# Attention scores from rounded fp32 in two passes, in a tuned trunk layer

## The chip, the cores and the metric

The kernel runs on one core of a Trainium2 chip. The metric is the device time of one execution in microseconds (us); the times of a kernel are given as the median of its runs.

## The reference

One layer of a trunk over 512 latent tokens with 256 context tokens, model width 1024, all in fp32. A normalised input is projected once into three branches (a gated width-3 convolution, a two-way diagonal state-space layer, and neighbourhood attention), which are gated, merged and projected; a squared-ReLU MLP with 4096 hidden columns follows. The change touches the scores of the attention alone:

```
s_loc = jnp.einsum('bqhd,bwkhd->bhqwk', q_r, k_r).astype(jnp.float32) * scale + bias
s_loc = jnp.where(key_in[:, None, :], s_loc, NEG_INF)
s_ctx = jnp.einsum('bqhd,bchd->bhqc', q_r, kch).astype(jnp.float32) * scale
s = jnp.concatenate([s_loc..., s_ctx], axis=-1)
p = jax.nn.softmax(s, axis=-1)
```

There are 8 heads of 64 channels. Each query sees a window of latent keys and all 256 context keys.

## The kernel before

Nearly all matrix products are made from *rounded fp32* (dtype fp32r, which PE takes in one pass, at some loss of low bits). To keep the precision, `split` (line 90) writes a value as a rounded high part and a rounded low part (the value less its high part), and `mm3` (line 98) adds three products into one accumulator: high x high, high x low, low x high (lines 99, 100, 101). Weights come from memory as a stream of 128 x 1024 blocks (`raw`); `wsplit` makes their high part on ACT (line 171) and their low part on DVE (line 174), two units ahead of use.

The work is a list of *units* (`unit_list`), one per 128 output columns. `slot` takes them in turn: it prepares weights for the unit after next, pumps the side streams, evacuates the unit before (`flush`, which calls `ev_unit`), and issues the unit's matmuls in two halves (`mm_unit`). The attention's units come as q, k, v for j = 0 to 3; each j holds two heads, one on partitions 0 to 63, the other on 64 to 127. A unit's result stands in one of three accumulators of 512 columns (`pm`, tag "m"); k and v take two each, one for the latent and one for the context tokens.

The attention itself is a side stream (`ATT.gen`, rate 3), in 16 steps n, four blocks i of 128 queries for each j. A step makes scores (line 788: two key ranges, a window of 192 or 256 keys and the 256 context keys, for each of the two heads), adds the bias with a running maximum (DVE, line 792), takes the exponential (ACT, line 801), transposes (line 814) and multiplies with v (line 829). The transposes of v are at line 754. The scores of before are plain fp32 matmuls over 64 rows of the array: q and k stand as fp32 tiles of 128 partitions, and each head uses its half of them. `ev_unit` writes these tiles: q by one ACT instruction (line 964), k by one on ACT (line 968) and one on DVE (line 969).

The order of each engine's instructions is fixed when the program is built: a planner takes, at each point of its own estimate of the run, the first instruction of the program order whose operands and buffers are ready. So side streams and units interleave on PE, and a changed instruction can change the order of others.

A "64 x 128" matmul here is one that uses 64 rows (input partitions) and 128 columns (output partitions) of PE's array; "128 x 64" one that uses all rows and half of the columns. The trace shows a plain fp32 score matmul as two instructions with two weight loads.

Of the kernel before, what the change touches and what calls it, by code (L numbers as in the profile page):

```python
# [9 lines left out]
F32 = mybir.dt.float32  # L10
F32R = mybir.dt.float32r
I32 = mybir.dt.int32
AF = mybir.ActivationFunctionType
# [3 lines left out]
MUL, ADD, SUB = ALU.mult, ALU.add, ALU.subtract  # L17

D = 1024
T = 512  # L20
# [55 lines left out]
def trunk(tc, xT, ctxT, cond, condT, vecs, wst, s5p, s5bc, dmat, biasA, outT):  # L76
# [3 lines left out]
    V, S, P, PE = nc.vector, nc.scalar, nc.gpsimd, nc.tensor  # L80

    def f(ap):
        return ap.bitcast(F32)
# [6 lines left out]
    def split(hi, lo, src, scale=None, eng=None):  # L90
        if scale is None:
            S.copy(hi, src)  # L92
            (eng or V).tensor_tensor(lo, src, f(hi), op=SUB)  # L93
        else:
            S.activation(hi, src, AF.Copy, scale=scale)
            V.scalar_tensor_tensor(lo, src, scale, f(hi), op0=MUL, op1=SUB)
# [7 lines left out]
    with es:  # L104
# [8 lines left out]
        def pm(name, n=T):  # L113
            return pp.tile([128, 512], F32, tag="m", bufs=3, name=name)[:, :n]

        def pa(name):
            return pp.tile([128, 1024], F32, tag="a", bufs=2, name=name)

        def pss(name):
            return pp.tile([128, 512], F32, tag="s", bufs=1, name=name)  # L120
# [38 lines left out]
        late = {}  # L159
# [39 lines left out]
        cs = cp.tile([128, 8, 2], F32, name="cs")  # L199
# [198 lines left out]
        for c in range(4):  # L398
# [7 lines left out]
            for t in range(4):  # L406
                o = 2 * t + c // 2
# [334 lines left out]
        qkv = {}  # L742

        class ATT:
# [19 lines left out]
            def gen(self):  # L764
                units = [(j, i) for j in range(4) for i in range(4)]
                bia = {}

                bt = [late["paf"].tile([128, 2, 512], F32, name=f"bt{e}") for e in range(2)]
                for t in bt:
                    P.memset(t[:, :, 256:512], 0.0)  # L770

                def load_bias(n):
                    if n < 16:
                        j, i = units[n]
                        t = bt[n % 2]
                        o = 2 * sum(NK[:i])
                        nc.sync.dma_start(t[:, :, 256 - NK[i]:256], biasA[j][:, o:o + 2 * NK[i]].rearrange("p (h m) -> p h m", h=2))
                        bia[n] = t

                def scores(n):  # L780
                    j, i = units[n]
                    nk, k0 = NK[i], K0[i]
                    q, k = qkv["q", j], qkv["k", j]
                    ps = pa(f"sps{n}").rearrange("p (h m) -> p h m", h=2)
                    for c0, c1, o in ((k0, k0 + nk, 256 - nk), (512, 768, 256)):
                        for h in range(2):
                            r = slice(64 * h, 64 * h + 64)
                            PE.matmul(ps[:, h, o:o + c1 - c0], q[r, 128 * i:128 * i + 128], k[r, c0:c1], start=True, stop=True)  # L788
                    mx = tp.tile([128, 4], F32, tag="mx", bufs=2, name=f"mx{n}")
                    for h in range(2):  # L790
                        sl = ps[:, h, 256 - nk:512]
                        V.tensor_tensor_reduce(out=sl, in0=sl, in1=bia[n][:, h, 256 - nk:512], scale=1.0, scalar=-3.0e38,
                                               op0=ADD, op1=ALU.max, accum_out=mx[:, h:h + 1])
                    V.tensor_scalar(mx[:, 0:2], mx[:, 0:2], -1.0, None, op0=MUL)
                    return ps, mx

                def soft(n, ps, mx):
                    nk = NK[units[n][1]]
                    pr = self.p.tile([128, 2, 512], F32, tag="pr", bufs=2, name=f"pr{n}")
                    for h in range(2):  # L800
                        self.ex[n] = S.activation(pr[:, h, 256 - nk:512], ps[:, h, 256 - nk:512], AF.Exp, bias=mx[:, h:h + 1], accum_out=mx[:, 2 + h:3 + h])
                    V.reciprocal(mx[:, 2:4], mx[:, 2:4])
                    for h in range(2):
                        V.tensor_scalar(pr[:, h, 256 - nk:512], pr[:, h, 256 - nk:512], mx[:, 2 + h:3 + h], None, op0=MUL)
                    return pr

                def transp(n, pr):
                    i = units[n][1]
                    nk = NK[i]
                    ps = pa(f"ptps{n}").rearrange("p (h t m) -> p h t m", h=2, t=4)  # L810
                    offs = (256 - nk, 128 if i != 3 else 192, 256, 384)
                    for h in range(2):
                        for t, o in enumerate(offs):
                            PE.transpose(ps[:, h, t], pr[:, h, o:o + 128], ident)  # L814
                    pt = self.p.tile([128, 2, 4, 128], F32, tag="pt", bufs=2, name=f"pt{n}")
                    S.copy(pt[:, 0], ps[:, 0])
                    V.tensor_copy(pt[:, 1], ps[:, 1])
                    return pt

                def values(n, pt):  # L820
                    j, i = units[n]
                    v = qkv["v", j]
                    ops = pss(f"ops{n}")[:, :128]
                    tiles = {0: ((0, 64), (1, 128)), 1: ((1, 128), (2, 128)), 2: ((2, 128), (3, 128)), 3: ((3, 128), (4, 64))}[i]
                    tiles += ((5, 128), (6, 128))
                    for t, (vt, rows) in enumerate(tiles):
                        for h in range(2):
                            r = slice(64 * h, 64 * h + 64)
                            PE.matmul(ops[r], v[:rows, vt, r], pt[:rows, h, t], start=t == 0, stop=t == 3, skip_group_check=True)  # L829
                    if i == 0:  # L830
                        self.of[j] = self.p.tile([128, 512], F32, tag="of", bufs=1, name=f"of{j}")
                    of = self.of[j]
                    S.copy(of[:, 128 * i:128 * i + 128], ops)
                    if i == 3:
                        split(*oo(j), of)

                load_bias(0)
                prev = None
                vps = None
                for n in range(17):  # L840
                    if n < 16:
                        while any((a, units[n][0]) not in qkv for a in ("vt", "q", "k")):
                            yield
                        load_bias(n + 1)

                    if vps is not None:
                        self.vsp(vps)
                        vps = None
                    if n < 16:
                        sc = scores(n)  # L850
                    if prev is not None:
                        pt = transp(n - 1, prev)
                    yield

                    if n < 16 and units[n][1] == 0:
                        vps = units[n][0]
                        self.vtr(vps)
                    if n < 16:
                        nxt = soft(n, *sc)
                    if prev is not None:  # L860
                        values(n - 1, pt)
                    prev = nxt if n < 16 else None
                    yield
# [4 lines left out]
        res = {}  # L868
# [11 lines left out]
        def oo(k):  # L880
            return gpair(6, 7, k) if k < 2 else hx(4 + k)
# [49 lines left out]
        def ev_unit(u):  # L931
            kind, j = u
            ps = res.get(u)
# [26 lines left out]
                    m = 2 * j + i  # L960
                    V.scalar_tensor_tensor(fg(m), gt["ga", m], 1.0, res[u, i], op0=ADD, op1=MUL)
            elif kind == "q":
                q = late["pa"].tile([128, T], F32, tag="q", bufs=2, name=f"q{j}")
                S.activation(q, ps, AF.Copy, scale=0.125)
                qkv[u] = q
            elif kind == "k":
                k = late["pa"].tile([128, 768], F32, tag="k", bufs=2, name=f"k{j}")
                S.copy(k[:, 0:512], ps)
                V.tensor_copy(k[:, 512:768], res[u, "c"])
                qkv[u] = k  # L970
            elif kind == "v":
                vt = tp.tile([128, 768], F32, tag="vt", bufs=1, name=f"vt{j}")
# [31 lines left out]
            elif kind == "m2":  # L1004
                c, m, h = j
# [91 lines left out]
        def flush():  # L1097
            if pending[0] is not None:
                u = pending[0]
                pending[0] = None  # L1100
                ev_unit(u)
# [20 lines left out]
        i = 0  # L1122
# [107 lines left out]
        for h, cs in enumerate(HALF):  # L1230
            for m in range(3, 8):
                ps = pm(f"wo{m}_{h}", 256)
# [5 lines left out]
        for h, cs in enumerate(HALF):  # L1238
# [11 lines left out]
            for j in range(4):  # L1250
# [3 lines left out]
                ps = pm(f"m1_{j}_{h}", 256) if j < 3 else pss(f"m1_{j}_{h}")[:, :256]  # L1254
# [9 lines left out]
        for h, cs in enumerate(HALF):  # L1264
            for m in (6, 7):
                ps = pm(f"m2e{m}_{h}", 256)
# [11 lines left out]
            else:  # L1278
# [8 lines left out]
                for t in range(2):  # L1287
                    ob = lp.tile([128, 1024], F32, tag="wl", bufs=3, name=f"ob{t}")
                    for e in range(2):
                        src, dst = ots[t][:, 512 * e:512 * e + 512], ob[:, 512 * e:512 * e + 512]  # L1290
# [145 lines left out]
```

## Time and profile before

| | us |
|---|---|
| median of 3 runs | 1051.85 (1051.36 to 1053.2) |
| the profiled execution | 1054.51 |
| its span in the trace | 1052.7 |

| engine | busy us | share of the span |
|---|---|---|
| PE (matmul) | 1004.4 | 95% |
| PEld (weight load) | 810.2 | 77% |
| DVE | 558.9 | 53% |
| ACT | 366.7 | 35% |
| POOL | 200.7 | 19% |

The span runs from the first to the last instruction of the program. PE's matmuls overlap in the trace (each one's duration includes its way through the array), so the time that a matmul takes from PE is read from start to start. The attention's matmuls lie between 434 and 610 us.

### The profile page before, as it was taken

What the parts mean: (1) busy time and instruction counts of PE and PEld (TensorE: products, weight loads), DVE (VectorE), ACT (ScalarE), POOL (GpSimd) and SP (SyncE); (2) the same over time, 40 slices, a digit from 0 to 9 for tenths busy, and PEclk for the clock granted to TensorE, in tenths of its full rate; (3) what the DMA queues carried; (4) which work ended last, traced back from release to release, by engine and by line L of the source; (5) the groups of instructions that cost most, each with busy time, mean ns of one, the idle gap of its engine ahead of it and who ended that gap; (6) DMA issues with size and microseconds to landing.
All of it is one profiled execution on the core that took longest, in us unless ns stands there. A gap on an engine that the chain in (4) does not pass through costs nothing.

```text
span 1052.7 us, 13485 instructions
## 1 busy us (share of the span) xinstructions
PE 1004.4 (95%) x5358; PEld 810.2 (77%) x5358; DVE 558.9 (53%) x927; ACT 366.7 (35%) x586; POOL 200.7 (19%) x159
## 2 busy tenths in 40 slices
PE   5889996989899999999999999999999999999997
PEld 2457885978788787777777778998888888888887
DVE  6733789348963144465467876566442234443322
ACT  5123422332222233354346444345331113333311
POOL 0555144546661013220020200000000000000000
PEclk9999999899799999999999999999999999999999
DMA  8355334785446456443254465223323223232202
GB/s 308 130 195 175 123 135 177 172 285 179 142 156 205 143 204 227 179 145 105 71 184 139 149 233 188 81 81 126 115 81 110 90 80 120 80 103 98 80 1 80
DMA packets 64543, 149.38 MB, mean 142 GB/s; under 512 B 28864, under 2 KB 41152, under 8 KB 52064
## 3 DMA queue, kind: packets, MB, share of 16 engines
q1 hardware_dynamic: 47792, 138.99, 38.4%
q10 hardware_dynamic: 16688, 9.53, 3.2%
q8 instruction: 42, 0.69, 0.3%
q14 instruction: 21, 0.17, 0.1%
HBM read 130.16 MB, written 18.32 MB: 141 GB/s over the span
## 4 chain that ended last, share of the span: by engine, by line
PE 74%; DMA 8%; DVE 8%; POOL 5%; issue 3%; ACT 2%; SPq 1%; ACTq 0%; DVEq 0%; POOLq 0%
PE m L99 10%; PE m L100 10%; PE m L101 10%; PE mod L511 3%; PE ops L829 2%; DMA raw<-in_wst_dram 2%; DMA C_d<-c 2%; PE sps L788 2%; PE ptps L814 2%; PE wo L100 1%; PE wo L99 1%; PE wo L101 1%; DVE v L681 1%; DVE wl L174 1%; DMA ks<-KT_d 1%
## 5 line engine op out<-in xcount | busy, mean ns | idle before, releaser
L174 DVE TENSOR_TENSOR wl<-raw,wh 128x1024 fp32r<-128x1024 f32 x144 | 187.6, 1303 | 226.1 <-ACT wh L171 224.4
L171 ACT CAST wh<-raw 128x1024 fp32r<-128x1024 f32 x144 | 150.9, 1049 | 314.6 <-PE m L100 151.1
L99 PE MATMUL m<-rg,wh 128*128 128x512 f32 (+1 forms) x480 | 184.2, 385 | 0.0
L101 PE MATMUL m<-rg,wl 128*128 128x512 f32 (+1 forms) x480 | 183.9, 384 | 0.0
L101 PEld LDWEIGHTS m<-rg,wl 128*128 128x128 f32 x480 | 90.1, 188 | 19.1
L99 PEld LDWEIGHTS m<-rg,wh 128*128 128x128 f32 x480 | 89.9, 188 | 18.7
L100 PE MATMUL m<-rg,wh 128*128 128x512 f32 (+1 forms) x256 | 96.4, 378 | 0.0
L100 PE MATMUL m<-actl,wh 128*128 128x512 f32 x224 | 87.8, 392 | 0.0
L1065 POOL TENSOR_TENSOR junk<-raw,silx 128x1024 f32<-128x1024 f32 x16 | 45.4, 2838 | 215.5 <-DMA raw<-in_wst_dram 214.2
L100 PEld LDWEIGHTS m<-rg,wh 128*128 128x128 f32 x256 | 48.0, 188 | 8.6
L511 PE MATMUL mod<-raw,cs 128*2 128x256 f32 x128 | 35.0, 432 | 17.9 <-DMA raw<-in_wst_dram 10.9
L100 PEld LDWEIGHTS m<-actl,wh 128*128 128x128 f32 x224 | 42.0, 187 | 9.8
L511 PEld LDWEIGHTS mod<-raw,cs 128*2 128x2 f32 x128 | 11.2, 92 | 38.1 <-issue 15.9
L1069 DVE SCALAR_TENSOR_TENSOR jk<-raw,silx 128x1024 bf16<-128x1024 f32 x16 | 21.8, 1362 | 32.5 <-DMA raw<-in_wst_dram 32.5
L1020 DVE SCALAR_TENSOR_TENSOR fg<-m,mod,fg 128x512 f32<-128x512 f32 x14 | 10.5, 751 | 52.8 <-PE m L101 52.8
L681 DVE TENSOR_TENSOR_SCAN v<-r,v 128x96 f32<-128x96 f32 x64 | 29.5, 523 | 15.1 <-POOL v L673 15.1
L92 ACT CAST rg<-relu 128x512 fp32r<-128x512 f32 (+1 forms) x36 | 20.3, 575 | 38.6 <-DVE relu L1013 38.6
L93 DVE TENSOR_TENSOR actl<-relu,rg 128x512 fp32r<-128x512 f32 (+1 forms) x36 | 22.3, 630 | 18.5 <-ACT rg L92 18.5
L100 PE MATMUL wo<-rg,wh 128*128 128x256 f32 (+1 forms) x104 | 31.8, 309 | 0.0
L99 PE MATMUL wo<-rg,wh 128*128 128x256 f32 (+1 forms) x104 | 31.8, 307 | 0.0
L101 PE MATMUL wo<-rg,wl 128*128 128x256 f32 (+1 forms) x104 | 31.5, 306 | 0.0
L829 PE MATMUL ops<-pt,v 128*64 128x128 f32 (+1 forms) x256 | 31.3, 287 | 0.0
(426 smaller groups left out, 2309.0 us busy)
## 6 DMA issues: line engine op xcount, KB each, us to landing
raw<-in_wst_dram SPq DMA_DIRECT2D x94, 1024.0 KB
E_d<-et ACTq DMA_DIRECT2D x8, 512.0 KB
C_d<-c SPq DMA_DIRECT2D x8, 512.0 KB
et<-E_d SPq DMA_DIRECT2D x8, 512.0 KB
ca<-C_d SPq DMA_DIRECT2D x8, 512.0 KB
fg<-in_xT_dram SPq DMA_DIRECT2D x4, 512.0 KB
raw<-in_wst_dram SPq DMA_DIRECT2D x4, 512.0 KB
u<-U_d SPq DMA_DIRECT2D x8, 256.0 KB
```

What stands on the lines that cost most here:

```text
L93: (eng or V).tensor_tensor(lo, src, f(hi), op=SUB)
L99: PE.matmul(ps, a[0], b[0], start=start, stop=False)
L100: PE.matmul(ps, a[0], b[1], start=False, stop=False)
L101: PE.matmul(ps, a[1], b[0], start=False, stop=stop)
L171: S.copy(a, src)
L174: V.tensor_tensor(b, src, f(a), op=SUB)
L511: PE.matmul(ps[0:2, 0:256], cs[:, kt], half(h)[:, 256 * (kt % 4):256 * (kt % 4) + 256], start=kt == 0, stop=kt == 7)
L681: V.tensor_tensor_scan(v[:, g, c], r8, v[:, g, c], 0.0, op0=MUL, op1=ADD)
L788: PE.matmul(ps[:, h, o:o + c1 - c0], q[r, 128 * i:128 * i + 128], k[r, c0:c1], start=True, stop=True)
L829: PE.matmul(ops[r], v[:rows, vt, r], pt[:rows, h, t], start=t == 0, stop=t == 3, skip_group_check=True)
L1065: P.tensor_tensor(junk, half(h), silx, op=MUL)
L1069: V.scalar_tensor_tensor(jk, half(h), 1.0, silx, op0=MUL, op1=MUL, accum_out=modx[:, i:i + 1])
```

## The change

`ev_unit` no longer writes q and k as plain fp32. For each head it makes a rounded q on both halves of the partitions (`q[:, h]`: the same high part twice), the low part of q on the head's own half (`ql`), and for k the high part on the head's half and the low part on the other half. The scores then take, for each range and head, one matmul over all 128 rows (high of q times high of k, plus high of q times low of k, in one pass), and one over the head's 64 rows (low of q times high of k) into the same accumulator.

```diff
-                    q, k = qkv["q", j], qkv["k", j]
+                    (q, ql), k = qkv["q", j], qkv["k", j]
...
                         for h in range(2):
                             r = slice(64 * h, 64 * h + 64)
-                            PE.matmul(ps[:, h, o:o + c1 - c0], q[r, 128 * i:128 * i + 128], k[r, c0:c1], start=True, stop=True)
+                            qs = slice(128 * i, 128 * i + 128)
+                            PE.matmul(ps[:, h, o:o + c1 - c0], q[:, h, qs], k[:, h, c0:c1], start=True, stop=False)
+                            PE.matmul(ps[:, h, o:o + c1 - c0], ql[r, qs], k[r, h, c0:c1], start=False, stop=True)
...
             elif kind == "q":
-                q = late["pa"].tile([128, T], F32, tag="q", bufs=2, name=f"q{j}")
-                S.activation(q, ps, AF.Copy, scale=0.125)
-                qkv[u] = q
+                q = late["pa"].tile([128, 2, T], F32R, tag="q", bufs=2, name=f"q{j}")
+                ql = late["pa"].tile([128, T], F32R, tag="ql", bufs=2, name=f"ql{j}")
+                for h in range(2):
+                    a, b = slice(64 * h, 64 * h + 64), slice(64 - 64 * h, 128 - 64 * h)
+                    S.activation(q[a, h], ps[a], AF.Copy, scale=0.125)
+                    V.scalar_tensor_tensor(ql[a], ps[a], 0.125, f(q[a, h]), op0=MUL, op1=SUB)
+                    S.activation(q[b, h], ps[a], AF.Copy, scale=0.125)
+                qkv[u] = q, ql
             elif kind == "k":
-                k = late["pa"].tile([128, 768], F32, tag="k", bufs=2, name=f"k{j}")
-                S.copy(k[:, 0:512], ps)
-                V.tensor_copy(k[:, 512:768], res[u, "c"])
+                k = late["pa"].tile([128, 2, 768], F32R, tag="k", bufs=2, name=f"k{j}")
+                for src, cs in ((ps, slice(0, 512)), (res[u, "c"], slice(512, 768))):
+                    for h in range(2):
+                        a, b = slice(64 * h, 64 * h + 64), slice(64 - 64 * h, 128 - 64 * h)
+                        S.copy(k[a, h, cs], src[a])
+                        V.tensor_tensor(k[b, h, cs], src[a], f(k[a, h, cs]), op=SUB)
                 qkv[u] = k
```

In the diff S is ACT, V is DVE and PE the matmul engine; `ps` is the unit's accumulator.

## Rows read from the trace of the kernel before

**Rows 1.** The page, its parts 1 (engines) and 4 (chain that ended last).

```profile
PE 1004.4 (95%) x5358; PEld 810.2 (77%) x5358; DVE 558.9 (53%) x927; ACT 366.7 (35%) x586; POOL 200.7 (19%) x159
...
PE 74%; DMA 8%; DVE 8%; POOL 5%; issue 3%; ACT 2%; SPq 1%; ACTq 0%; DVEq 0%; POOLq 0%
```

**Rows 2.** Busy us by stage: slices, their sum 400:640, sum 600:1053; clock, DMA last.

```profile
400.00:420.00 20.00, 17.73 (x73) 14.23 (x72) 9.59 (x7) 8.35 (x13) 7.48 (x3) 0.91 0.53 186
...
440.00:460.00 20.00, 20.00 (x117) 14.95 (x116) 11.83 (x26) 10.51 (x21) 5.21 (x2) 1.00 0.48 163
460.00:480.00 20.00, 20.00 (x136) 15.89 (x134) 13.93 (x26) 13.72 (x26) 3.43 (x1) 1.00 0.36 118
...
sum 240.00, PE 237.25 PEld 179.97 DVE 150.56 ACT 110.05 POOL 39.57; mean PE 19.77 PEld 15.00 DVE 12.55 ACT 9.17 POOL 3.30
...
sum 453.00, PE 446.68 PEld 378.55 DVE 206.84 ACT 149.04 POOL 0.56; mean PE 34.36 PEld 29.12 DVE 15.91 ACT 11.46 POOL 0.04
```

**Rows 3.** PE's waits, 400 to 640 us: total us, times, longest us.

```profile
PE k L99 <- ACT q L964: 2.3, 1, 2.3
```

**Rows 4.** Busy us of instructions on score tiles, 434:592: PE, PEld, DVE, ACT; clock, DMA.

```profile
434.00:592.00 158.00, 21.92 (x128) 12.10 (x128) 20.00 (x30) 20.93 (x60) 1.00 0.39 131
```

**Rows 5.** PE in order of time (start, us), a step whose scores stand apart.

```profile
433.76 0.39 PE L99 MATMUL q<-rg,wh 128*128 128x512 f32 x1
...
434.44 0.39 PE L99 MATMUL q<-rg,wh 128*128 128x512 f32 x1
434.76 0.59 PE L788 MATMUL sps<-k,q 64*128 64x192 f32 x2
435.28 0.50 PE L100 MATMUL q<-rg,wh 128*128 128x512 f32 x1
435.71 0.59 PE L788 MATMUL sps<-k,q 64*128 64x192 f32 x2
436.23 0.50 PE L101 MATMUL q<-rg,wl 128*128 128x512 f32 x1
```

**Rows 6.** PE in order of time, a step whose scores stand together, and the last.

```profile
445.69 0.39 PE L101 MATMUL k<-rg,wl 128*128 128x512 f32 x1
446.01 1.13 PE L788 MATMUL sps<-k,q 64*128 64x256 f32 x8
447.07 0.38 PE L99 MATMUL k1c<-rg,wh 128*128 128x256 f32 x1
447.29 0.28 PE L100 MATMUL k1c<-rg,wh 128*128 128x256 f32 x1
...
447.53 0.40 PE L99 MATMUL k<-rg,wh 128*128 128x512 f32 x1
...
590.69 1.03 PE L788 MATMUL sps<-k,q 64*128 64x192 f32 x8
```

**Rows 7.** Weight loads in order of time, the first after those scores.

```profile
447.07 0.19 PEld L99 LDWEIGHTS k1c<-rg,wh 128*128 128x128 f32 x1 [0.33 <-issue]
```

**Rows 8.** PE in order of time, two shapes by turns.

```profile
457.00 0.43 PE L829 MATMUL ops<-pt,v 128*64 128x128 f32 x2
457.37 0.33 PE L814 MATMUL ptps<-ident,pr 128*128 128x128 f32 x1
457.63 0.43 PE L829 MATMUL ops<-pt,v 128*64 128x128 f32 x2
```

**Rows 9.** By line: ns min/median/max, first and last start, forms.

```profile
L964 ACT ACTIVATE q<-q x4: 589/592/607, 412.6 to 522.8; 128x512 f32<-128x512 f32 x4
...
L969 DVE COPY k<-k1c x1: 424/424/424, 451.8 to 451.8; 128x256 f32<-128x256 f32 x1
...
L93 DVE TENSOR_TENSOR rg<-of,rg x4: 678/686/694, 488.5 to 610.4; 128x512 fp32r<-128x512 f32 x4
...
L997 DVE SCALAR_TENSOR_TENSOR tgc<-tgc,na x8: 677/680/689, 623.7 to 642.8; 128x512 f32<-128x512 f32 x8
```

**Rows 10.** ACT in order of time, right after the first q.

```profile
413.12 1.07 ACT L954 ACTIVATE tgc<-gc 128x512 f32<-128x512 f32 x2
```

## The prediction

> **What bounds the kernel now.** I read the page first. Its first part has PE busy for 95% of the span against 53% for DVE and 35% for ACT, and in its fourth part PE holds 74% of the chain that ended last [rows 1]. The change touches only the attention stretch, so I looked at that by stage next: from 400 to 640 us PE is busy 237.25 of 240 us at a granted clock of 1.00 in all but the first slice, while DVE has 150.56 and ACT 110.05 us [rows 2]. The waits of PE in the same stretch are then short: the longest is one of 2.3 us on the evacuation of q [rows 3]. So in this stretch PE's own stream sets the time, and what the change adds to that stream or takes from it reaches the end nearly one to one. Nothing later gives it back: from 600 us to the end PE is busy 446.68 of 453 us [rows 2], and weights are fetched only as earlier ones are used up.
>
> The reader should then look inside that stream. A busy PE is not a streaming PE: start-to-start times show where it waits for itself [rows 5, 6, 8].
>
> **The change part by part.**
>
> *1. What a score matmul costs now.* Line 788 runs 64 times (16 units, two key ranges, two heads); the trace has 128 instructions for it, two per matmul, each 64 rows by 128 columns of the array [rows 4]. Full-array rounded matmuls give the pace of a column: three of 512 columns take 0.68 us from start to start (433.76 to 434.44), 0.227 each, and two of 256 take 0.24 (447.29 to 447.53), 0.12 each [rows 5, 6], so 0.42 ns a column and some 12 ns each.
>
> Contiguous: in rows 6 the eight instructions of a unit start at 446.01, and the next matmul at 447.07. From the start of the matmul before them (445.69) to the second one after them (447.29) it is 1.60 us; less those two neighbours at their usual 0.227 and 0.12, the unit costs 1.25 us. The eight instructions run two at a time (the heads sit on different halves of the rows), and four times 2 x 256 columns x 0.42 ns are 0.86; that each column passes twice per instruction is what makes this and the next paragraph agree. The other 0.39 is spent on entering and leaving the 64-row shape, 0.20 each. A unit with a 192-key range streams 64 columns less in two of the four, 2 x 2 x 64 x 0.42 = 0.11 less, so 1.15.
>
> Alone: in rows 5 the period from one full matmul to the next with one score matmul of 192 between is 0.95 us. Less 0.227 for the full one and 0.32 for the score (2 instructions x 2 x 192 columns x 0.42 ns), 0.40 is left for two changes of shape, again 0.20 each. So a lone score matmul costs 0.72 (192) or 0.83 (256).
>
> The 128 instructions stand in 25 runs, the first at 434.76 and the last at 590.69 [rows 5, 6]. Twelve units stand whole (7 x 1.25 + 5 x 1.15 = 14.5), two are in four lone pieces (2 x 3.1 = 6.2), one in three pieces (2.5), one in two (1.9). Sum before: 25.1 us. The busy time that the trace gives these instructions, 21.92 us [rows 4], counts their own and not the neighbours' stretch, and fits.
>
> *2. What the new score matmuls cost.* There are 128 again: 64 on all 128 rows (call them F) and 64 on 64 rows (L). All are rounded fp32, one pass. Streaming: 96 of 256 columns x 0.12 + 32 of 192 x 0.09 (0.12 less 64 columns) = 14.4 us. But the program order is F, L, F, L, and F needs all rows. Two heads no longer run beside each other, and each L is alone between full-array matmuls, whoever is put between: each pays two changes of shape, 64 x 0.39 = 25.0 us. Sum after: 39.4 us, so **+14.3 us** on PE. Per whole unit, 2.5 replaces 1.25; for the units that already stand in lone pieces it is nearly even.
>
> The nearest row for such an alternation: from 457.00 to 457.63 one pair of value matmuls (128 x 64 shape) and one transpose (128 x 128) of 128 columns each take 0.63 us [rows 8], and 0.11 of that is streaming. Two changes of shape cost 0.52 there, more than I take. The clock stayed at 1.00 through it [rows 2], so I add nothing for the clock.
>
> Bounds of the change of shape: at the top, 0.26 each by rows 8, 64 x 0.52 = 33.3, so +22.6. At the bottom nothing: every 64-row matmul in this trace is also plain fp32, and if the gap belonged to the format and not to the shape, all of it would go: 14.4 - 25.1 = -10.7. I take 0.39 per L, from the rows nearest to it (64 x 128 shape next to rounded full-array matmuls). Rows 8 speak for shape: there both sides are plain fp32 and the gap is there all the same. PE's weight loads say it too: after the scores the next load starts only after 0.33 us idle, put down to issue [rows 7], not prefetched as the others are.
>
> [...]
>
> The rounded matmul of 192 columns: no rounded one under 256 columns is in the trace. Low end 0.09 (by columns), high end 0.32, the plain-fp32 price above; 32 of them, so 0 to +7.4. I take 0, since 256 and 512 go by columns.
>
> *3. Evacuations.* q: one ACT instruction (0.59 us) becomes four, plus two DVE subtractions; k: one ACT and one DVE become four and four [rows 9]. A half-partition instruction costs by its columns, so at most 0.59 each on ACT and 0.69 on DVE (lines 93 and 997 are the same kinds). Per j at most 6 x 0.59 = 3.5 us more of ACT and, with the 256-wide ones at 0.42, 3.2 us more of DVE; four j: 14 and 13 us beside 110.05 and 150.56 of 240 [rows 2]. What hides it: PE has 12 or more matmuls of the next unit queued (2.8 us) while a pair of accumulators is read, and scores come a whole unit (v) after k. Behind these evacuations in the in-order queues stand the weight casts (lines 171 and 174), which are prepared two units ahead. I cost all of this at nothing but for the place below; if that cover is gone, each of the 8 evacuations shows up as some 2 us.
>
> One place has no cover: the first k matmul waits on q's evacuation for 2.3 us [rows 3]. ACT starts that one at 412.6 [rows 9] and the next at 413.12 [rows 10], 0.5 apart; four of them and the last subtraction end about 1.7 later. Between 0 (if the planner puts a gate's evacuation first) and +1.8; I take **+1.5**.
>
> *4. SBUF.* The attention pool grows by 14 KB a partition (q and k doubled, ql new, two buffers each). Its tiles wait for the same closed pools as before: 0.
>
> **Sum.** +14.3 + 1.5 = +15.8 us. The profiled execution took 1054.51 us (span 1052.7, and 1.8 around it), 2.7 above the median of the timed ones, 1051.85. So 1070 for a profiled one and **1068 us** for the median.
>
> **The rivals.**
>
> *A. The gap belongs to the format, and goes.* -10.7 + 1.5 = -9.2: 1043. For it: no rounded 64-row matmul is in the trace. Against it: rows 8, and that the rounded neighbours in rows 5 are themselves stretched.
>
> *B. The two L of a range come to stand together* (F, F, L, L: the planner moves the second F ahead, or PE does). They then share one visit and run beside each other: streaming 14.4 - 3.6 = 10.8, changes of shape 32 x 0.39 = 12.5, sum 23.3, so -1.8 + 1.5: 1052, no change. The point from which it decides: with some 33 visits or fewer in place of 64 (0.39 + 0.11 each) the kernel is not slower. For it: the planner does interleave streams in places [rows 5, 8]. Against it: the three matmuls of a split product keep their program order (lines 99, 100, 101) in rows 5 and 6, whatever is put between.
>
> *C. The narrow rounded matmul is dear:* +15.8 + 7.4: 1075.
>
> *D. ACT and DVE set the time:* eight evacuations open a wait of 2 us each in place of the one: +14.3 + 16: 1082. For it: DVE is busy 11.8 to 13.9 of 20 us at 440 to 480 [rows 2]. Against it: in the same slices PE was busy all 20 us [rows 2].
>
> **How the numbers follow.** Forecast 71%, with its own range 1061 to 1073 (0.35 to 0.47 per L; the planner's order of everything after may move by 3 us). A 7%, B 9%, C 8%, D 5%. The range of 8 in 10 takes the forecast's range and C, and part of the dearer change of shape: 1057 to 1076. About 0.2%, 2 us, is what a measurement of this kernel can tell from no change. Faster: A and a third of B, 10%. Same: half of B and the forecast's low tail, 6%. Slower: 84%.
>
> **What would show it.** Right: line 788 becomes two lines of 64 instructions; start to start, each L and the F after it take about 0.6 us (256 columns); the attention stretch is about 15 us longer with PE as busy as before; ACT and DVE have some 12 us more and PE waits for neither save at the first k. Wrong: an L 0.12 us after its F (A); two L starting some 10 ns apart (B); the 192-column ones slower than the 256 (C); PE waiting on line 964's or 968's successors at each j (D).

## The result, and the profile after

The changed kernel takes 1063.78 us (median of 4 runs, 1063.27 to 1065.94), the kernel before 1052.53 beside it (4 runs): a ratio of 1.011, 95% interval 1.0093 to 1.0126. It is slower by 11.3 us, less than the 15.8 us of the forecast (1068). Its profiled execution took 1063.27 us, the one of the kernel before 1054.51, with spans of 1061.5 and 1052.7: the two traces are 8.8 us apart, 2.5 less than the medians, so what follows explains 8.8 us.

The page of the changed kernel, engines and chain, answers to [rows 1]: PE has 11 us more, DVE 13.5 and ACT 12, and PE's share of the chain grows.

```profile
PE 1015.8 (96%) x5358; PEld 822.1 (77%) x5358; DVE 572.4 (54%) x947; ACT 378.7 (36%) x610; POOL 198.1 (19%) x159
...
PE 78%; DVE 8%; DMA 5%; POOL 4%; issue 2%; SPq 1%; ACT 1%; DVEq 0%; ACTq 0%; POOLq 0%
```

By stage (the columns of [rows 2]), two slices and the sum from 400 to 640 us: PE is as full as before (237.93 us against 237.25), beside more DVE and ACT.

```profile
440.00:460.00 20.00, 20.00 (x109) 15.09 (x108) 16.73 (x31) 12.88 (x26) 4.53 (x2) 1.00 0.50 170
460.00:480.00 20.00, 20.00 (x116) 15.02 (x114) 10.89 (x20) 10.65 (x20) 3.42 (x1) 1.00 0.26 86
...
sum 240.00, PE 237.93 PEld 183.23 DVE 157.13 ACT 118.42 POOL 36.05; mean PE 19.83 PEld 15.27 DVE 13.09 ACT 9.87 POOL 3.00
```

PE's waits in the same stretch (total us, times, longest), for [rows 3]. There is one (before had a second of 0.4 us, at line 754). A gate's evacuation now stands where q's stood.

```profile
PE k L99 <- ACT tgc L956: 2.1, 1, 2.1
```

PE in order of time, a whole unit of scores (F is line 789, L line 790), for [rows 6]. The first L is 0.21 us after its F, and from there each F and each L is 0.31 us after the one before it; the pace of 256 columns is 0.117.

```profile
443.51 0.40 PE L99 MATMUL k<-rg,wh 128*128 128x512 f32 x1
443.75 0.28 PE L789 MATMUL sps<-k,q 128*128 128x256 f32 x1
443.96 0.38 PE L790 MATMUL sps<-k,ql 64*128 64x256 f32 x1
444.27 0.38 PE L789 MATMUL sps<-k,q 128*128 128x256 f32 x1
444.58 0.38 PE L790 MATMUL sps<-k,ql 64*128 64x256 f32 x1
...
445.83 0.38 PE L790 MATMUL sps<-k,ql 64*128 64x256 f32 x1
446.14 0.50 PE L100 MATMUL k<-rg,wh 128*128 128x512 f32 x1
446.48 0.40 PE L101 MATMUL k<-rg,wl 128*128 128x512 f32 x1
```

From 443.51 to 446.48 are 2.97 us; less the two 512-column neighbours at 0.227, the unit costs 2.5, as forecast.

**Where the time went.** The first k matmul starts at 413.3 us in both kernels, the first one after the attention (unit `na`) at 619.2 and 628.0. PE in order of time, before and then after:

```profile
413.27 0.50 PE L99 MATMUL k<-rg,wh 128*128 128x512 f32 x1 [2.27 <-ACT q L964]
...
619.20 0.39 PE L99 MATMUL na<-rg,wh 128*128 128x512 f32 x1
```

```profile
413.25 0.50 PE L99 MATMUL k<-rg,wh 128*128 128x512 f32 x1 [2.07 <-ACT tgc L956]
...
627.96 0.39 PE L99 MATMUL na<-rg,wh 128*128 128x512 f32 x1
```

So the whole of the 8.8 us by which the spans differ lies in this stretch. I added up PE's time there, each instruction from its start to the start of the next:

| us (from the two traces) | before | after |
|---|---|---|
| stretch | 205.9 | 214.7 |
| score matmuls | 20.2 | 36.8 |
| values | 28.0 | 24.9 |
| transposes of the probabilities | 15.5 | 13.5 |
| projections (q, k, v, `la`, `lb`) | 139.1 | 136.7 |
| transposes of v | 3.2 | 2.9 |
| steps from a value matmul to a transpose or back | 38: 8.5 | 15: 3.3 |

Counted with the neighbours that they stretch, steps that begin or end at a score go from 27.6 us (153) to 44.3 (167); the 14 further ones would have taken some 0.2 each anyway, so the scores cost **+13.9 us**. (The table's own line, without the neighbours, gives +16.6; how a change of shape between a score and its neighbour is shared out moves the figure by one or two us.) Some 5 us came back at values and transposes, whose order the planner changed: the rows by turns of [rows 8] are rarer.

### The profile page after: what moved, and what is told of

It reads as the page before. It is cut to its first block, busy times and chain, and to the rows that moved or that the text cites. A ratio compares the mean times of both kernels' runs of the same rounds, so it can differ in the third digit from the quotient of the medians.

```text
span 1061.5 us, 13539 instructions
## 1 busy us (share of the span) xinstructions
PE 1015.8 (96%) x5358; PEld 822.1 (77%) x5358; DVE 572.4 (54%) x947; ACT 378.7 (36%) x610; POOL 198.1 (19%) x159
## 4 chain that ended last, share of the span: by engine, by line
PE 78%; DVE 8%; DMA 5%; POOL 4%; issue 2%; SPq 1%; ACT 1%; DVEq 0%; ACTq 0%; POOLq 0%
PE m L99 10%; PE m L100 10%; PE m L101 10%; PE mod L511 3%; PE ops L831 2%; DMA C_d<-c 2%; PE sps L790 2%; DVE v L681 2%; PE ptps L816 1%; PE sps L789 1%; PE wo L99 1%; PE wo L100 1%; PE wo L101 1%; DVE wl L174 1%; PE gc L101 1%
## 5 line engine op out<-in xcount | busy, mean ns | idle before, releaser
L171 ACT CAST wh<-raw 128x1024 fp32r<-128x1024 f32 x144 | 150.9, 1049 | 321.5 <-PE m L100 146.6
L1077 POOL TENSOR_TENSOR junk<-raw,silx 128x1024 f32<-128x1024 f32 x16 | 42.3, 2642 | 226.7 <-DMA raw<-in_wst_dram 225.4
L92 ACT CAST rg<-relu 128x512 fp32r<-128x512 f32 (+1 forms) x36 | 20.2, 575 | 38.5 <-DVE relu L1025 38.5
L1081 DVE SCALAR_TENSOR_TENSOR jk<-raw,silx 128x1024 bf16<-128x1024 f32 x16 | 23.9, 1495 | 15.8 <-DMA raw<-in_wst_dram 15.7
L794 DVE CUSTOM_DVE_ANT_0 sps<-sps,bt 128x448 f32<-128x448 f32 (+1 forms) x32 | 21.2, 664 | 20.6 <-PE sps L790 20.2
```

Of the source, the lines that this page charges most:

```text
L171: S.copy(a, src)
L1077: P.tensor_tensor(junk, half(h), silx, op=MUL)
L1081: V.scalar_tensor_tensor(jk, half(h), 1.0, silx, op0=MUL, op1=MUL, accum_out=modx[:, i:i + 1])
```

## The experiments

Later sessions spread more: the kernel before had medians of 1053.1 to 1054.3 us in them (1049 to 1063 in all). Each ratio below, with its 95% interval, is against runs of the kernel before taken alongside; the stretch and the waits are those of one profiled execution.

**1. L on all 128 rows.** The low part of q is written to both halves.

```diff
-PE.matmul(ps[:, h, o:o + c1 - c0], ql[r, qs], k[r, h, c0:c1], start=False, stop=True)
+PE.matmul(ps[:, h, o:o + c1 - c0], ql[:, h, qs], k[:, h, c0:c1], start=False, stop=True)
...
-V.scalar_tensor_tensor(ql[a], ps[a], 0.125, f(q[a, h]), op0=MUL, op1=SUB)
+V.scalar_tensor_tensor(ql[a, h], ps[a], 0.125, f(q[a, h]), op0=MUL, op1=SUB)
+V.scalar_tensor_tensor(ql[b, h], ps[a], 0.125, f(q[a, h]), op0=MUL, op1=SUB)
```

> The second score matmul takes all 128 rows too: the low part of q is written on both halves of the partitions (two more DVE subtractions per q) and multiplied with high and low of k, so no 64-row matmul is left. Theory (the time went into changes of the array's shape, 0.39 us for each of 64 visits): the scores cost 128 streams, 96 x 0.12 + 32 x 0.09 = 14.4 us, 10.7 less than the kernel before; the order also visits the 128 x 64 shape of the value matmuls 40 times in place of 47, at 0.42 us 3 us less. 1039 us, at most 1042; each second matmul starts 0.12 us after the first. Rival 1 (the rounded accumulation itself, not the shape, is slow): about 1060, like the changed kernel. Rival 2 (DVE, now with 5 us more of evacuation work than in the changed kernel, sets the time): above 1048.

Measured: 1046.7 us, ratio 0.9934 (0.9899 to 0.9969). In order of time in this run, F and L are now 0.12 us apart, and the unit takes 0.95 us from its first start to the next matmul, in place of 2.39 (443.75 to 446.14 above):

```profile
440.49 0.28 PE L789 MATMUL sps<-k,q 128*128 128x256 f32 x1
440.61 0.28 PE L790 MATMUL sps<-k,ql 128*128 128x256 f32 x1
...
441.44 0.39 PE L100 MATMUL k<-rg,wh 128*128 128x512 f32 x1
```

So the price belongs to the change of shape. But the run misses its expectation: the stretch is 199.8 us where its working (205.9 less 10.7 for the scores and 3 for the values) gives 192.2. Beside the one at the first k, PE's waits in it are new, these two the longest:

```profile
PE ptps L816 <- DVE pr L806: 2.1, 2, 1.7
PE v L99 <- ACT q L973: 1.3, 1, 1.3
```

**2. Four F, then four L.** Only the order in a unit is changed; the two heads' L can stand side by side.

```diff
-for c0, c1, o in ((k0, k0 + nk, 256 - nk), (512, 768, 256)):
-    for h in range(2):
...
+parts = [(c0, c1, o, h) for c0, c1, o in ((k0, k0 + nk, 256 - nk), (512, 768, 256)) for h in range(2)]
+for c0, c1, o, h in parts:
+    PE.matmul(ps[:, h, o:o + c1 - c0], q[:, h, qs], k[:, h, c0:c1], start=True, stop=False, ...)
+for c0, c1, o, h in parts:
+    PE.matmul(ps[:, h, o:o + c1 - c0], ql[r, qs], k[r, h, c0:c1], start=False, stop=True, ...)
```

> Same instructions as the changed kernel, but within a unit the four full-array matmuls come first, then the four of 64 rows. In the planned order the 64-row shape is visited 26 times in place of 64, the 128 x 64 shape 35 times as in the changed kernel. Theory: visits 26 x 0.39 = 10.1 us, full-array streams 7.2, 64-row streams side by side 3.6 to 5, so 21 to 22 us for the scores against 39: 17 to 18 less than the changed kernel, 1046 us (1044 to 1049). Two 64-row matmuls of a unit start some 10 ns apart. Rival 1 (each 64-row rounded matmul pays its own entry, whoever stands before it): 1063. Rival 2 (the evacuations hold PE up as soon as its stream is shorter): between, with waits of PE on ACT or DVE in the rows.

Measured: 1046.48 us, ratio 0.9951 (0.9917 to 0.9985), as expected. In order of time, a unit from 440.70 to 441.69:

```profile
440.70 0.63 PE L788 MATMUL sps<-k,q 128*128 128x256 f32 x4
441.26 0.50 PE L791 MATMUL sps<-k,ql 64*128 64x256 f32 x4
441.69 0.50 PE L100 MATMUL k<-rg,wh 128*128 128x512 f32 x1
```

Visits to the 64-row shape are 26 in place of 64, and two L of different heads start 4 to 5 ns apart. The unit takes 0.99 us, as against 2.39 in the changed kernel. The loss of the change is its order F, L, F, L, not its two passes.

**3. The evacuations alone.** The new evacuations write plain fp32, and the scores stay those of before.

```diff
-PE.matmul(ps[:, h, o:o + c1 - c0], q[:, h, qs], k[:, h, c0:c1], start=True, stop=False)
-PE.matmul(ps[:, h, o:o + c1 - c0], ql[r, qs], k[r, h, c0:c1], start=False, stop=True)
+PE.matmul(ps[:, h, o:o + c1 - c0], q[r, h, qs], k[r, h, c0:c1], start=True, stop=True)
...
-q = late["pa"].tile([128, 2, T], F32R, tag="q", bufs=2, name=f"q{j}")
+q = late["pa"].tile([128, 2, T], F32, tag="q", bufs=2, name=f"q{j}")
...
-k = late["pa"].tile([128, 2, 768], F32R, tag="k", bufs=2, name=f"k{j}")
+k = late["pa"].tile([128, 2, 768], F32, tag="k", bufs=2, name=f"k{j}")
```

> The evacuations of the changed kernel (four ACT and two DVE instructions per q, four and four per k), but into plain fp32 tiles, and the plain fp32 64-row scores of the kernel before. The low parts come out as zeros and are not used. Theory (the extra 14 us of ACT and 13 us of DVE are hidden behind PE): within 2 us of the kernel before, and if anything less, since the order visits the 64-row shape 21 times in place of 25: 1051. Rival (the evacuations carry part of the 11 us): 1056 or more, with waits of PE on lines of the q and k evacuation.

Measured: 1056.13 us, ratio 1.0023 (0.9996 to 1.005); the stretch is 207.4 us, 1.5 more than before. PE's waits in it:

```profile
PE ptps L815 <- DVE pr L805: 3.2, 3, 1.7
PE k L99 <- ACT tgc L955: 2.1, 1, 2.1
PE lb L99 <- ACT rg L1191: 1.5, 1, 1.5
```

None is on an evacuation of q or k, against the rival, though the time is the rival's (1056 or more) and not the 1051 of the theory: by the ratio it is 2.4 us longer, -0.4 to 5.3. Of the 3.2 us on the scaling of the probabilities (line 805), 2.6 stand behind two scalings that took 2.38 and 2.34 us in place of 0.46, each beside a product on POOL; run 5 shows what that is. So the longer evacuations cost little here, and by what way is not shown.

**4. The scores alone.** The new matmuls, on operands written by the short evacuations of before.

```diff
-PE.matmul(ps[:, h, o:o + c1 - c0], q[r, 128 * i:128 * i + 128], k[r, c0:c1], start=True, stop=True)
+qs = slice(128 * i, 128 * i + 128)
+PE.matmul(ps[:, h, o:o + c1 - c0], q[:, qs], k[:, c0:c1], start=True, stop=False)
+PE.matmul(ps[:, h, o:o + c1 - c0], ql[r, qs], k[r, c0:c1], start=False, stop=True)
...
-q = late["pa"].tile([128, T], F32, tag="q", bufs=2, name=f"q{j}")
+q = late["pa"].tile([128, T], F32R, tag="q", bufs=2, name=f"q{j}")
 S.activation(q, ps, AF.Copy, scale=0.125)
-qkv[u] = q
+qkv[u] = q, q
...
-k = late["pa"].tile([128, 768], F32, tag="k", bufs=2, name=f"k{j}")
+k = late["pa"].tile([128, 768], F32R, tag="k", bufs=2, name=f"k{j}")
```

(against the kernel before)

> The F, L, F, L scores of the changed kernel, with the short evacuations of the kernel before (one ACT for q, one ACT and one DVE for k, rounded). The operands are not the right ones: both heads' channels are summed and the low part of q is replaced by its high part. Theory (PE's visits to the 64-row shape alone make the change): 64 visits and 39 visits of the value shape, so as slow as the changed kernel, 1062 to 1066. Rival (the evacuations are part of it): halfway back, 1056 to 1059.

Measured: 1065.5 us, ratio 1.0125 (1.0084 to 1.0166), as expected: the scores alone make the whole change. What comes back at values and transposes comes back here, too (64 visits to the 64-row shape; values and transposes take 38.8 us, before 43.5).

**5. Low part zeroed on its second half**, to see whether run 1's miss is DVE's work.

```diff
-V.scalar_tensor_tensor(ql[b, h], ps[a], 0.125, f(q[a, h]), op0=MUL, op1=SUB)
+P.memset(f(ql[b, h]), 0.0)
```

(against run 1)

> The low part of q takes all 128 rows as in the run with two subtractions more, but the second half of it is zeros, written by POOL, so DVE has 8 subtractions fewer in the stretch; the product is high of k times low of q, as in the changed kernel, and no score matmul has a shape of its own. Theory (what kept the earlier run at 1046.7 instead of 1039 is DVE's work and the order that came with it: PE waited 2.1 us on DVE at the transposes, 1.3 us on ACT at v, and the clock fell after one of these waits): 1041 us, 1038 to 1044; attention stretch 191 to 196 us in place of 199.8, and these waits gone. Rival (the shortfall is the price of a shorter stretch: bias, exponentials and weights come no faster, whoever writes the low part): 1045 to 1048, stretch 198 to 201, the same waits at other places.

Measured: 1046.1 us, ratio 0.9916 (0.9885 to 0.9946), stretch 199.6: time and stretch are those that the rival of this run gave. (The profiled execution, 1051.0 us, was the longest of its eight.) Its trace then shows what holds PE up, which is not the length of the softmax alone. Here are its DVE, POOL and PE in order of time around one wait, and the granted clock of three windows (after the busy times):

```profile
463.27 1.22 DVE L1082 SCALAR_TENSOR_TENSOR jk<-raw,silx 128x1024 bf16<-128x1024 f32 x1 [1.92 <-DMA raw<-in_wst_dram]
...
464.62 3.13 DVE L806 TENSOR_SCALAR pr<-pr,mx 128x512 f32<-128x512 f32 x2
```

```profile
463.31 3.41 POOL L1078 TENSOR_TENSOR junk<-raw,silx 128x1024 f32<-128x1024 f32 x1 [9.65 <-DMA raw<-in_wst_dram]
```

```profile
467.15 1.94 PE L816 MATMUL ptps<-ident,pr 128*128 128x128 f32 x8 [2.06 <-DVE pr L806]
468.74 0.56 PE L101 MATMUL v1c<-rg,wl 128*128 128x256 f32 x1
469.10 0.41 PE L99 MATMUL v1c<-rg,wh 128*128 128x256 f32 x1
469.32 0.41 PE L100 MATMUL v1c<-rg,wh 128*128 128x256 f32 x1
```

```profile
464.00:465.00 1.00, 1.00 (x10) 0.89 (x8) 0.96 (x4) 0.99 (x3) 1.00 (x1) 1.00 0.01 2
467.20:470.20 3.00, 3.00 (x15) 3.00 (x16) 2.40 (x7) 1.86 (x5) 0.95 (x2) 0.50 0.84 254
471.00:474.00 3.00, 3.00 (x16) 2.50 (x15) 2.58 (x7) 2.84 (x7) 0.00 (x0) 1.00 0.22 78
```

The first scaling of the probabilities takes 2.38 us where 0.46 is usual, and ends 0.3 us after the POOL product that runs beside it. The transposes wait 2.06 us for the scalings, and then PE's granted clock is 0.50 in place of 1.00 for 3 us, which costs another 1.5 (an estimate, half of the 3). In the kernel before, three scalings are held in the same way (463.0, 545.9 and 598.4 us); there PE has other work at that moment. So are five in run 1, four in run 3 and two each in runs 8 and 10, and in each of these PE's longest wait on the scaling (1.7, 1.7, 1.9 and 1.4 us) comes right behind one of them.

**6 and 7. Values without a shape of their own.** Each head's value matmuls use all 128 columns of the array, in the kernel before (6) and in the changed one (7).

```diff
-ops = pss(f"ops{n}")[:, :128]
+ops = pss(f"ops{n}")[:, :256].rearrange("p (h m) -> p h m", h=2)
...
-PE.matmul(ops[r], v[:rows, vt, r], pt[:rows, h, t], start=t == 0, stop=t == 3, skip_group_check=True)
+PE.matmul(ops[:, h], v[:rows, vt], pt[:rows, h, t], start=t == 0, stop=t == 3, skip_group_check=True)
...
-S.copy(of[:, 128 * i:128 * i + 128], ops)
+for h in range(2):
+    r = slice(64 * h, 64 * h + 64)
+    S.copy(of[r, 128 * i:128 * i + 128], ops[r, h])
```

> The kernel before, with the value matmuls over all 128 columns of the array, each head into columns of its own in the accumulator (of which half is used). The 128x64 shape is gone, but two heads no longer run side by side: a unit of values streams 16 x 0.109 us in place of 8 x 0.109, so 16 units x 0.87 = +13.9 us; of 94 changes of shape at the values some 16 stay (the 64-row tiles), 78 x 0.2 = -15.6 us. Expected 1050, 1046 to 1054. What matters is the difference from the changed kernel with the same edit: see there.

> The changed kernel with the same edit of the values. +13.9 us of streaming; of its 70 changes of shape at the values some 16 stay, 54 x 0.2 = -10.8. Theory (the 5 us by which the change came out cheaper than its +14.3 us of scores are changes of the values' shape, which the planner's new order saves): without that shape nothing is left to save, so the step from the kernel before to the changed one widens from 8.8 to about 14 us (12.5 to 16) with this edit in both, and this run takes 1064 to 1068. Rival (the 5 us come from elsewhere, a better overlap of the projections or transposes): the step stays at 8 to 10 us, about 1059.

Measured: 1054.36 us (ratio 1.001, 0.9983 to 1.0037) and 1065.13 (1.0109, 1.0066 to 1.0153). The step between them is 10.8 us: between the two expectations, and with these intervals it tells nothing. Values and transposes take 46.0 us and 44.7, so 1.3 come back here in place of 5, as the theory has it; but run 6 has waits that run 7 lacks (2.0 us on DVE at the values, 2.5 at `lb` and `la`, and 4.6 at the first k against 2.5), and its profiled execution, 1061.77 us, was 7 us above its median, so the pair isn't clean.

**8 and 9. Values together**, each kernel's own matmuls, but preferred by the planner: in the kernel before (8) and in the changed one (9).

```diff
+with tc.high_priority(offset=30):
     PE.matmul(ops[r], v[:rows, vt, r], pt[:rows, h, t], start=t == 0, stop=t == 3, skip_group_check=True)
```

> The kernel before, computing the same, with the value matmuls preferred by the planner, so that a unit's values stand together: steps from a value matmul to a transpose or back fall from 38 to 3, visits to the 128x64 shape from 47 to 32; the scores' visits stay (25, 26 here). Theory (the changed kernel got some 5 us back because its order has fewer visits to the values' shape): 15 visits x 0.4 = 6 us off: 1046 us, 1044 to 1049, the attention stretch 199 to 202 us in place of 205.9. Rival (values and transposes by turns cost nothing, since the turns fill time in which PE would wait for the probabilities; the 5 us are from elsewhere): 1050 to 1054, and waits of PE on ACT and DVE at lines of the softmax that the kernel before does not have.

> The same preference in the changed kernel: visits to the values' shape from 35 to 31, steps between values and transposes from 15 to 5. Theory: 4 x 0.4 = 1.6 us off, 1062 us (1060 to 1064), so that between this run and the one before it, with nearly the same number of visits at the values, the scores' price shows whole: 13 to 16 us. Rival: the step between the two stays at 9 to 11 us.

Measured: 1056.25 us, ratio 0.9992 (0.9963 to 1.0021), and 1062.68, ratio 1.0075 (1.0045 to 1.0105). The theory's gain of 6 us in run 8 is not there. The step between the two is 8.7 us by the ratios and by the stretches (206.4 and 215.0) and 6.4 by the medians: not the 13 to 16 of the theory, and at or under the rival's 9 to 11. In run 8 the steps between values and transposes did fall (8.5 us to 0.6), and the stretch stayed at 206.4 us, because PE's waits came in their place, 9.4 us in all. Its five longest, and then the only one of run 9, in which PE has the 14 us of scores more:

```profile
PE ptps L814 <- DVE pr L804: 3.0, 2, 1.9
PE ptps L814 <- ACT junk L1067: 2.2, 1, 2.2
PE k L99 <- ACT q L965: 1.8, 1, 1.8
PE ops L830 <- DVE pt L817: 0.9, 1, 0.9
PE ops L830 <- ACT pt L816: 0.9, 1, 0.9
```

```profile
PE k L99 <- ACT tgc L957: 2.3, 1, 2.3
```

So in the kernel before the turns fill time in which PE would wait for the softmax. In run 8, 1.9 of the 3.0 us on line 804 stand behind a scaling that POOL's product held, and the 2.2 us are ACT's, at a sum of such a product; whether the 6 us would show without these products was not run.

**10. Runs 2 and 8 together** (the two edits shown there).

> Four full-array score matmuls, then the four of 64 rows, as in the earlier run (1046.5), with the values together as well: visits to the values' shape 35 to 31, so 1.6 us off by the theory, 1045 (1042 to 1047). With DVE and ACT as busy as they are there, waits of 1 to 2 us at the transposes or values can eat this: 1046 to 1049 by the rival.

Measured: 1046.5 us, ratio 0.9916 (0.9885 to 0.9947), stretch 200.9 (run 2: 197.7): nothing gained on run 2. The time lies in the ranges of both; the waits and the stretch speak for the rival. PE waits 1.4 us on line 807, 0.7 on 804.

**11 and 12. Run 5 without POOL's products** (11), and with these products on DVE (12), each against run 5.

```diff
 if i % 2:
-    P.tensor_tensor(junk, half(h), silx, op=MUL)
-    S.activation(junk, junk, AF.Identity, accum_out=modx[:, i:i + 1])
+    S.activation(junk, half(h), AF.Identity, accum_out=modx[:, i:i + 1])
```

```diff
-if i % 2:
+if False:
     P.tensor_tensor(junk, half(h), silx, op=MUL)
```

> The run with the low part of q zeroed on its second half (1046.1), and POOL's 16 products of a side stream (line 1078) left out: ACT sums the raw weights in place of the products, so the modulation is not the reference's. In that run PE waited 2.1 us on the scaling of the probabilities by DVE (line 806): this one took 2.38 us in place of 0.46, and ended 0.3 us after a POOL product that ran beside it; PE then ran at half rate for 3 us; and ACT waited 28.5 us in all for POOL's products, with evacuations and exponentials behind it. Theory (POOL's products hold DVE and ACT, and so the softmax, once PE's own stream is short): without them no scaling takes over 0.6 us, PE's waits on the softmax shrink from 3.5 us to under 1, the stretch goes from 199.6 to 192 to 196, the time to 1039 to 1043. Rival (the softmax chain itself is too long, products or not): 1045 to 1048, and PE waits on other lines of it.

> The same, but with POOL's products and ACT's sums done by DVE, as the other half of these products already is (16 more of 1.23 us): a kernel that computes the reference. Theory: DVE has some 17 us more in the stretch (171 before) but is never held by POOL: 1041 to 1045. Rival: with DVE at some 188 of 240 us its own queue delays the softmax: 1046 to 1050, PE waits on DVE at lines 806 and 819.

Measured: 1042.97 us, ratio 0.989 (0.9854 to 0.9926), and 1041.68, ratio 0.9873 (0.983 to 0.9916), both in the range that the theory gives; the stretches are 193.9 and 194.4 us, against 199.6 in run 5. By the medians that is 3.1 and 4.4 us less than run 5, with intervals that overlap its own; that its waits on the scaling are gone is clearer than the size of the gain. In run 11 no scaling takes over 0.49 us, and PE waits at the first k alone. By line, the scaling in run 5 and then in run 12 (ns min/median/max):

```profile
L806 DVE TENSOR_SCALAR pr<-pr,mx x32: 445/464/2415, 446.1 to 595.4; 128x448 f32<-128x448 f32 x16, 128x512 f32<-128x512 f32 x16
```

```profile
L806 DVE TENSOR_SCALAR pr<-pr,mx x32: 445/466/827, 446.4 to 583.0; 128x448 f32<-128x448 f32 x16, 128x512 f32<-128x512 f32 x16
```

PE's waits of run 12 in the stretch, and its sum by stage:

```profile
PE sps L789 <- ACT pr L803: 0.8, 1, 0.8
PE v L99 <- ACT q L973: 0.6, 1, 0.6
```

```profile
sum 240.00, PE 238.56 PEld 194.36 DVE 170.07 ACT 111.61 POOL 2.26; mean PE 19.88 PEld 16.20 DVE 14.17 ACT 9.30 POOL 0.19
```

DVE took over POOL's products (26 in the stretch in place of 13) and is no busier than in run 5 (170.69 us): an instruction that is held counts as busy, and the longest scaling is now one of 0.83 us, beside POOL's zeros. Both runs take away two holds at once, DVE's and ACT's wait for the products; which of them counted more is not shown. Run 12 has the lowest median here. Whether the kernel before, or the changed one, gains by the same edit was not run.

## Why the prediction was right, and where it was off

*What bounds the kernel.* Right for what is added to PE: the change's +13.9 us of scores all lie on the path. Too simple for what is taken away: in runs 1, 5, 8 and 10, with less work for PE, it waits for the softmax on DVE and ACT, and the gain on the kernel before stays at some 6 to 8 us (none in run 8) until POOL's products are taken off (runs 11 and 12, 11 to 12 us). So "nearly one to one" held for what this change adds, and not for what the runs take away.

*Scores: +14.3 forecast, +13.9 measured.* The price of 0.39 for each visit to the 64-row shape held for rounded operands: 0.31 us for each of F and L against 0.117 makes 0.2 for each change. Run 1 shows that it is the shape, run 2 that matmuls of one shape side by side share it. The changes became more, as the sum had it: 64 visits against 25, at some 0.2 us for each change. What PE does in that time, no trace shows. The upper bound of 0.26 came from a slip in reading [rows 8]: it takes 0.11 of the 0.63 us as streaming, but in the kernel before a transpose starts 0.109 us after the one before it, and a pair of values 0.109 after the pair before it, so 0.22 is streaming and 0.20 is left for each change there, too. A rounded matmul of 192 columns takes 0.11 us (run 1, below) and not the 0.09 of the sum, 0.6 us over all 32.

*The first k: +1.5 forecast, -0.2 measured* (and the matmul starts at the same time, 413.3). This term failed. The planner put a gate's evacuation ahead of q's, the case given as the lower bound, and the wait is 2.1 us against 2.3.

*Evacuations at nothing: held, within some 2 us.* ACT and DVE have 12 and 13.5 us more; run 4 shows the change whole without the longer evacuations (ratio 1.0125, the change 1.011), and run 3, with them alone, is 2.4 us longer than the kernel before, with an interval that includes no change (-0.4 to 5.3).

*What was missing:* some 5 us that came back at the values and transposes. The forecast had the planner's order as a spread of 3 us, not as a term. How it came about is argued, not shown: in the kernel before, PE bridges the softmax with values and transposes by turns, at 0.2 us for each change of shape; with more scores to do it needs fewer of these turns (38 steps to 15). That the saved steps alone are worth nothing without work to take their place, run 8 shows. What makes the planner choose one order or the other was not traced, and runs 6 and 7 could not confirm the amount.

In the stretch, which begins at the first k, 13.9 - 5.1 gives the 8.8 us between the two traces. This divides up one difference and is no check of it; what tests the 13.9 are runs 1, 2 and 4. The measured 1063.8 lies in the range of 1057 to 1076, but nearer to the 1068 than the terms deserve: with the two that were off put right (-1.5 and -5) the sum gives 1061 or 1062, and the medians happen to stand 2.5 us further apart than the traces. That part of the hit is luck.

*The rivals.* A (the gap belongs to the format) fell: a rounded L pays 0.2 a change. B (pairs of L) did not happen in the changed kernel, 64 visits. Run 2 goes further than B, with four L side by side and 26 visits: it gives 1046.5 where B's sum gave 1052, and some 4 us come back at values and transposes there, too. C fell: the first score in the changed kernel, 192 columns, stands 0.18 us before the L that follows it, with a change of shape in between, and in run 1, with no such change, 192 columns after 192 take 0.11:

```profile
428.78 0.25 PE L789 MATMUL sps<-k,q 128*128 128x192 f32 x1
428.96 0.35 PE L790 MATMUL sps<-k,ql 64*128 64x192 f32 x1
```

```profile
462.15 0.27 PE L790 MATMUL sps<-k,ql 128*128 128x192 f32 x1
462.26 0.28 PE L789 MATMUL sps<-k,q 128*128 128x192 f32 x1
462.38 0.27 PE L790 MATMUL sps<-k,ql 128*128 128x192 f32 x1
```

D fell: no wait of PE on q's or k's evacuation in the changed kernel.

## What to carry to other kernels

Count the changes of the array's shape, not the passes: a matmul of half the rows between full ones pays 0.4 us here, more than three times its streaming, and a matmul over all rows, with zeros on the idle ones, takes it away (run 5), the grouping of equal shapes most of it (run 2). An engine that is 99% busy tells what added work costs, not what removed work saves: look for the chain that becomes late next, and expect the order around the edit to pay back a part of what you add. When an instruction takes several times its median, look at what the neighbouring engine does in those microseconds.

## What the runs showed of the hardware

POOL's two-input product (2.3 to 3.4 us) holds some DVE instructions and leaves others alone. Of those that begin while it runs, from 400 to 640 us of the kernel before and of run 5, the scaling in SBUF (0.46 us) takes 1.0 to 2.4, the weights' low part (line 174, two inputs in SBUF, 1.22 us) 2.6 to 3.4, while the bias step on PSUM keeps its 0.63 to 0.70 and the copies from PSUM their 0.55 and 0.69 (all us). In the kernel before, a held scaling ends 0.25 to 0.29 us after the product, the low part 1.08 us after it; without the products no scaling takes over 0.49 us (run 11). By what way the product holds them, no trace shows.

After a wait of 2.06 us PE was granted 0.50 of its clock for 3 us (run 5). Not after every wait of that length: after one of 2.17 us in run 8 the granted clock was 1.00 (552.5 to 555.5 us).
